# A quarter of one output projection moved behind the transposes, and the sample's projection parts joined in pairs

## The chip, the cores and the metric

The kernel runs on one core of one Trainium2 chip. The metric is the device time of one execution in microseconds (us); the median of three runs of the kernel before is 2836.79 us. Five engines work side by side, each in its own order: PE (matrix products, also transposes), DVE (vector), ACT (scalar), POOL (general), and SP, which here only issues the loads and stores (DMAs). They wait for each other by semaphores.

## The reference

One inference step of a one-layer decoder, all in fp32, for a prompt of 2048 tokens and a sample of 8 requests with 4 new tokens each (32 tokens). The width is 1024. Cut to what matters here:

```
y    = concatenate([o, s_out]) @ w_out          # o: gated linear attention, s_out: spatial gating
h    = x + y
q    = rmsnorm(h, g_x) @ wq_x                   # memory cross-attention, 4 heads, 256 memory tokens
h    = h + softmax(q @ mk.T / 16) @ mv @ wo_x   # mk, mv: from mem_prompt, or cache_mem_k/v for the sample
f    = (gelu(conv(rmsnorm(h, g_ffn) @ w_gate)) * (rmsnorm(h, g_ffn) @ w_up)) @ w_down     # d_ff 2816
h    = h + f
out  = rmsnorm(h, g_final)
```

`o` is normalized per head and multiplied by silu(r) before it enters `w_out`: rows 0 to 511 of `w_out` belong to `o`, rows 512 to 1023 to `s_out`.

## The kernel before

The 2048 prompt tokens are four sub-blocks of 512 (s = 0 to 3). The 32 sample tokens ride along with sub-block 1 through the mixer, so there T = 544, cut in two chunks of 272 columns. Activations lie transposed, 128 features by tokens; `B.h[0..7]` is the residual. Every fp32 product is three fp32r matmuls (`mm3`, L92 to L94): high times high, high times low, low times high. A weight unit is 512 KB, loaded raw by SP and split on chip by ACT (high part, L84) and DVE (low part, L85), unless it was prepared in DRAM before. Raw units share 5 buffers (`wraw`), split ones 5 each of high and low.

The work is a list of `Step`s, each with a function and the weight units that it reads. `weave` mixes main steps with side steps in proportion; `run` issues them in that order and asks for units 5 ahead (`AHEAD`). The Tile framework then schedules the instructions with a timeline of its own, so the final order on each engine can differ from the written one; the order of an engine's instructions is fixed when the program is built.

The change touches two places of sub-block 1.

*The output projection `wo`* (`out_proj_steps`). `half(m2, k0, last)` multiplies 4 of the 8 tiles of the reduction (from k0) for two of the 8 output tiles (m = 2·m2, 2·m2+1) and adds the result to `B.h[m]` (L1240). For sub-block 1 `first` is 4 and `second` is 0: the four halves with k0 = 4 read `s_out` and can run early; the four with k0 = 0 read `o`, and they finish a tile (`finish`: scaling wog L1250, the combinations t13, t24 and splits for the attention scores, the copy smpx for the sample L1260, squares on ACT L1262 and their sum on POOL L1267). The first list is woven with the tail of the linear attention (`gtail`, main steps 16 to 18: normalization of `o`, the gate L1181, `back`: transposes otp L1187 and, for the sample, otps L1192, each scaled and split into ch by ACT, L88, and cl by DVE, L89). The second list follows, then the statistics and the attention scores sc (matmuls into `sc10A..`, `sc10S..`, against splits of the finished pairs: w1, wth/wtl, wbh/wbl, wuh/wul with the number of the pair's odd tile, so `w1wo17` and `wthwo17` belong to tiles 6 and 7). Matmuls into `a_wo1<k0><m><chunk>` are these projections: `a_wo146x` and `a_wo147x` are the fourth half with k0 = 4, `a_wo100x` the first with k0 = 0.

*The sample's cross-attention* (`sample_steps`). Its steps run beside the feed-forward of sub-block 1 (main steps 1 to 37): project with `wq_x` ("sq"), then per request keys, scores, softmax, values, then project with `wo_x` ("so"). A projection is a sum over two halves j of the reduction for four column blocks m, in plain fp32 with 32x256 matmuls (L1406) into sqp or sop; each half reads one raw unit of 512 KB, `r_sq<m><j>` or `r_so<m><j>`. Raw units of the feed-forward, `r_wup1<j>S..`, share those buffers.

Of the kernel before, what the change touches and what calls it, by code (L numbers as in the profile page):

```python
# [37 lines left out]
def hymba_step_kernel(  # L38
# [22 lines left out]
    def U(name, dt=F32):  # L61
        return up.tile([128, TM], dt, tag="U", name=name)

    def T_(name, dt=F32):
        return tp_.tile([128, TM], dt, tag="T", name=name)
# [4 lines left out]
    def acc(name):  # L70
        return accp.tile([128, 512], F32, tag="acc", name=name)
# [7 lines left out]
    def const(shape, name, dt=F32):  # L79
        return cp.tile(shape, dt, tag=name, name=name)  # L80
# [10 lines left out]
    def mm3(ps, wh, wl, xh, xl, first, last):  # L91
        pe.matmul(ps, wh, xh, start=first, stop=False)  # L92
        pe.matmul(ps, wh, xl, start=False, stop=False)  # L93
        pe.matmul(ps, wl, xh, start=False, stop=last)  # L94
# [4 lines left out]
    def wload(w, k0, nk, m0, mw, name):  # L99
        raw = wraw(name)  # L100
        r3 = raw[:, :nk * mw].rearrange("p (k m) -> p k m", k=nk)
        nc.sync.dma_start(r3, w[k0 * 128:(k0 + nk) * 128, m0:m0 + mw].rearrange("(k p) m -> p k m", p=128))
        return r3
# [11 lines left out]
    def wraw_unit(*spec):  # L115
        return lambda: wload(*spec)
# [64 lines left out]
    def seven_tokens(a, b, H, name, apart=False):  # L181


        B11, B12, B21, B22 = a[:, :H], a[:, H:2 * H], b[:, :H], b[:, H:2 * H]
        t13, t24 = T_(f"t13{name}"), T_(f"t24{name}")
        lo_, hi_ = slice(0, H), slice(H, 2 * H)
        one = U(f"w1{name}", F32R)
        split(one[:, lo_], one[:, hi_], B11)
        out = {"A11": (one[:, lo_], one[:, hi_])}
        dve.tensor_tensor(t13[:, lo_], B12, B11, ALU.subtract)  # L190
        th, tl = U(f"wth{name}", F32R), U(f"wtl{name}", F32R)
        if apart:
            split(th[:, lo_], tl[:, lo_], t13[:, lo_])
        dve.tensor_tensor(t13[:, hi_], B22, B12, ALU.subtract)
        dve.tensor_tensor(t24[:, lo_], B22, t13[:, lo_], ALU.subtract)
        dve.tensor_tensor(t24[:, hi_], B21, t24[:, lo_], ALU.subtract)
        for nm, src, first, second in (("b", b, "A12", "S4"), ("u", t24, "S2", "A22"), ("t", t13, "S1", "S3")):
            if nm == "t":
                h, l, c = th, tl, slice(H if apart else 0, 2 * H)
            else:  # L200
                h, l, c = U(f"w{nm}h{name}", F32R), U(f"w{nm}l{name}", F32R), slice(0, 2 * H)
            split(h[:, c], l[:, c], src[:, c])
            out[first], out[second] = (h[:, lo_], l[:, lo_]), (h[:, hi_], l[:, hi_])
        return out
# [153 lines left out]
    for l in range(7):  # L358
        half = 1 << l
# [6 lines left out]
        m = const([128, 256], f"mask{l}", U8)  # L366
# [32 lines left out]
    def gcol(nm, k):  # L399
        return cols_of[nm][:, k:k + 1]  # L400
# [273 lines left out]
    def chunks_of(sample):  # L674
        return [(0, 272), (272, 272)] if sample else [(0, 512)]
# [535 lines left out]
    def out_proj_steps(B, unit, src, g, name, sample, first, finished, keep=None, seven=False,  # L1211
                       whole=False):

        s = B.s
        T = TM if finished else SB
        TH = SB if keep else T

        open_ = {}

        def half(m2, k0, last, begin=True, end=True):

            def fn(wu):
                wh, wl = wu
                x = src()
                if m2 == 0 and last:
                    B.hn, B.sq = [], None
                for mm in range(2):  # L1230
                    m = 2 * m2 + mm
                    ms = slice(mm * 128, (mm + 1) * 128)
                    for ci, (c0, cw) in enumerate(chunks_of(sample)):
                        cs = slice(c0, c0 + cw)
                        ps = acc(f"a_{name}{s}{k0}{m}{ci}") if begin else open_.pop(m)
                        for k in range(4):
                            mm3(ps[:, :cw], wh[:, k, ms], wl[:, k, ms], x[k0 + k][0][:, cs], x[k0 + k][1][:, cs],
                                begin and k == 0, end and k == 3)
                        if end:
                            dve.tensor_tensor(B.h[m][:, cs], ps[:, :cw], B.h[m][:, cs], ALU.add)  # L1240
                        else:
                            open_[m] = ps
                    if last:
                        finish(m)
            return Step(fn, [unit(k0, m2)])

        def finish(m):
            if seven:
                t = T_(f"{name}g{s}{m}")
                act.activation(t[:, :TH], B.h[m][:, :TH], AF.Copy, scale=gcol(g, m))  # L1250
                if m % 2:
                    B.hn.append(seven_tokens(B.even, t, TH // 2, f"{name}{s}{m}", name == "wo" and m == 7))
                else:
                    B.even = t
            else:
                hi, lo = U(f"{name}h{s}{m}", F32R), U(f"{name}l{s}{m}", F32R)
                split_scaled(hi[:, :TH], lo[:, :TH], B.h[m][:, :TH], gcol(g, m))
                B.hn.append((hi, lo))
            if keep:
                dve.tensor_scalar(keep()[:, m * NS:(m + 1) * NS], B.h[m][:, SB:TM], gcol(g, m), None, ALU.mult)  # L1260
            t = T_(f"{name}q{s}{m}")
            act.activation(t[:, :T], B.h[m][:, :T], AF.Square)  # L1262
            if m == 0:
                B.sq = U(f"{name}sq{s}")
                pool.tensor_copy(B.sq[:, :T], t[:, :T])
            else:
                pool.tensor_tensor(B.sq[:, :T], B.sq[:, :T], t[:, :T], ALU.add)  # L1267

        def stat():
            ps = mps(f"{name}ss{s}")  # L1270
            rs = narrow(f"{name}rs{s}")
            for c in range(5 if finished else 4):
                n = 128 if c < 4 else NS
                pe.matmul(ps[:n, c:c + 1], B.sq[:, c * 128:c * 128 + n], ones[:, 0:1], start=True, stop=True)
            rstd_of(rs[:, :4], ps[:, :4], 128, 4, 1.0 / D)
            if finished:
                rstd_of(rs[:NS, 4:5], ps[:NS, 4:5], NS, 1, 1.0 / D)
            B.rs = rs

        second = 4 - first  # L1280
        if whole:
            out = [half(m2, first, False, end=False) for m2 in (0, 1)]
            out += [half(m2, second, True, begin=False) for m2 in (0, 1)]
            for m2 in (2, 3):
                out += [half(m2, first, False, end=False), half(m2, second, True, begin=False)]
            return out[:2], out[2:], Step(stat)
        return ([half(m2, first, False) for m2 in range(4)], [half(m2, second, True) for m2 in range(4)], Step(stat))


    def attention_steps(B):  # L1290
# [93 lines left out]
    def sample_steps():  # L1384
# [12 lines left out]
        def project(w, of, got, name):  # L1397


            st = {}  # L1400

            def part(m, j, raw):
                if m % 2 == 0 and j == 0:
                    st["ps"] = mps(f"{name}p{m}")
                for k in range(4):
                    pe.matmul(st["ps"][hr[k], (m % 2) * 256:(m % 2 + 1) * 256], of(4 * j + k), raw[:, k],  # L1406
                              start=j == 0, stop=j == 1)
                if m % 2 and j:
                    t = T_(f"{name}t{m}")
                    dve.tensor_copy(t[:, :512], st["ps"])  # L1410
                    if m == 1:
                        st["f"] = mps(f"{name}f")
                    for i in range(4):
                        a = ((m // 2) * 4 + i) * NS
                        pe.matmul(st["f"][:, a:a + NS], t[:, i * 128:(i + 1) * 128], sum4, start=True, stop=True)
                    if m == 3:
                        got(st["f"])

            return [Step(lambda a, m=m, j=j: part(m, j, a), [wraw_unit(w, 4 * j, 4, m * 256, 256, f"{name}{m}{j}")])
                    for m in range(4) for j in range(2)]  # L1420

        def got_q(ps):
            smp.qs = U("sqs")
# [85 lines left out]
        out = []  # L1509
# [260 lines left out]
    for s, B in enumerate(blocks):  # L1770
# [6 lines left out]
        if B.mix_sample:  # L1777
            def keep():
                if not hasattr(smp, "x"):
                    smp.x = U("smpx")  # L1780
                return smp.x
        w1, w2, stat = out_proj_steps(B, lambda k0, m2, s=s: (w_out[0], k0, 4, m2 * 256, 256, f"wo{s}{k0}{m2}"),
                                      lambda B=B: B.cat, "gx", "wo", B.mix_sample, 4, B.mix_sample, keep, seven=True, whole=not B.mix_sample)
# [59 lines left out]
```

## Time and profile before

| | before |
|---|---|
| median of 3 runs (range) | 2836.79 us (2836.49 to 2840.41) |
| profiled execution | 2837.18 us |
| its span | 2835.5 us |
| PE busy | 2797.1 us (99%) |
| DVE, ACT, POOL busy | 1894.6 (67%), 1106.0 (39%), 569.5 us (20%) |
| mean granted PE clock | 0.995 |
| DMA | 638.21 MB, 225 GB/s in the mean |

Times in the profile count from the span's start. A timeline row gives start, duration, engine, line, operation, output <- inputs and, in brackets, the idle time before it with the instruction that ended it. A wait row reads "engine, output, line <- what ended the wait: total, times, longest". Matmuls overlap: a row's duration is longer than the distance to the next one, and the distance is what PE needs for it.

### The profile page before, as it was taken

How to read it: one execution, taken by the hardware profiler on the slowest of the kernel's cores; microseconds unless marked ns; L12 is line 12 of the kernel's file. 1: busy time of each engine (PE TensorE's matmuls, PEld its weight loads, DVE VectorE, ACT ScalarE, POOL GpSimd, SP SyncE). 2: the span in 40 equal slices, each digit the busy share in tenths (PEclk: the TensorE clock that was granted, in tenths of full speed). 3: DMA queues.
4: the chain of work that ended last, by engine and by line, in shares of the span. 5: the costliest groups of instructions: out<-in, count | busy, mean ns of one | idle time of the engine just before them, and what ended most of it. 6: DMA issues, size and time to landing. Idle time of an engine off the chain costs nothing.

```text
span 2835.5 us, 47052 instructions
## 1 busy us (share of the span) xinstructions
PE 2797.1 (99%) x17894; PEld 2477.9 (87%) x17894; DVE 1894.6 (67%) x3266; ACT 1106.0 (39%) x1950; POOL 569.5 (20%) x638
## 2 busy tenths in 40 slices
PE   8999999999999999999999999999999999999998
PEld 8888888888887898898888889899999888899997
DVE  6578778777657786655555778666666687665555
ACT  5645544333363354223124445422223544431222
POOL 2002213111111221322210121222221022132222
PEclk9999999999999999999999999999999999999999
DMA  9756589999932245888995216577776323677774
GB/s 297 250 182 219 180 267 341 336 343 329 337 112 68 85 154 195 314 288 291 331 324 190 82 60 208 194 252 258 258 269 207 112 69 128 206 260 273 272 281 177
DMA packets 369687, 638.21 MB, mean 225 GB/s; under 512 B 27370, under 2 KB 238412, under 8 KB 369462
## 3 DMA queue, kind: packets, MB, share of 16 engines
q1 hardware_dynamic: 369462, 635.20, 65.7%
q8 instruction: 142, 2.33, 0.3%
q14 instruction: 83, 0.68, 0.1%
HBM read 507.69 MB, written 127.41 MB: 224 GB/s over the span
## 4 chain that ended last, share of the span: by engine, by line
PE 63%; DVE 3%; ACT 1%; issue 0%; POOL 0%; DMA 0%; POOLq 0%; DVEq 0%; ACTq 0%
PE d L94 4%; PE d L92 4%; PE d L93 4%; PE a_wx L94 2%; PE a_wx L93 2%; PE a_wx L92 2%; PE a_wo L92 1%; PE s L1046 1%; PE a_wo L93 1%; PE a_wo L94 1%; PE a_wu L92 1%; PE a_wu L93 1%; PE t_wr L92 1%; PE t_wr L93 1%; PE a_wu L94 1%; PE t_wr L94 1%
## 5 line engine op out<-in xcount | busy, mean ns | idle before, releaser
L92 PE MATMUL d<-acth,whi_wd 128*128 128x272 f32 (+1 forms) x688 | 235.4, 342 | 0.0
L1692 DVE TENSOR_TENSOR h<-d,h 128x512 f32<-128x512 f32 (+1 forms) x232 | 133.7, 582 | 149.4 <-PE d L94 149.2
L94 PE MATMUL d<-acth,wlo_wd 128*128 128x272 f32 (+1 forms) x688 | 233.4, 340 | 0.0
L93 PE MATMUL d<-actl,whi_wd 128*128 128x272 f32 (+1 forms) x688 | 233.3, 339 | 0.0
L1589 POOL TENSOR_TENSOR c<-c,bc_f 128x512 f32<-128x512 f32 (+1 forms) x88 | 137.0, 1562 | 140.4 <-ACT c L1588 139.7
L1579 ACT ACTIVATE c<-g,colsb 128x512 f32<-128x512 f32 x88 | 71.7, 815 | 189.7 <-DVE g L1542 141.7
L94 PEld LDWEIGHTS d<-acth,wlo_wd 128*128 128x128 f32 x688 | 129.5, 188 | 15.5 <-issue 1.2
L93 PEld LDWEIGHTS d<-actl,whi_wd 128*128 128x128 f32 x688 | 129.5, 188 | 13.5 <-issue 0.4
L92 PEld LDWEIGHTS d<-acth,whi_wd 128*128 128x128 f32 x688 | 129.6, 188 | 13.1
L1611 POOL TENSOR_TENSOR c<-r_q_wup,c 128x512 f32<-128x512 f32 (+1 forms) x33 | 63.3, 1918 | 329.4 <-DVE r_q_wup L288 209.6
L92 PE MATMUL a_wo<-ch,h_wo 128*128 128x512 f32 (+1 forms) x320 | 114.3, 369 | 2.0 <-ACT r L876 1.3
L1576 POOL COPY carry<-g 128x2 f32<-128x2 f32 x88 | 29.5, 335 | 420.8 <-DVE g L1542 418.8
L93 PE MATMUL a_wo<-cl,h_wo 128*128 128x512 f32 (+1 forms) x320 | 113.8, 358 | 0.0
L94 PE MATMUL a_wo<-ch,l_wo 128*128 128x512 f32 (+1 forms) x320 | 112.9, 356 | 0.0
L1580 DVE SCALAR_TENSOR_TENSOR c<-g,colsb,c 128x512 f32<-128x512 f32 x88 | 84.9, 965 | 28.3 <-ACT c L1579 27.8
L94 PE MATMUL a_wx<-pTh,wlo_wx 128*128 128x512 f32 x256 | 101.3, 396 | 0.0
L93 PE MATMUL a_wx<-pTl,whi_wx 128*128 128x512 f32 x256 | 100.6, 393 | 0.0
L92 PE MATMUL a_wx<-pTh,whi_wx 128*128 128x512 f32 x256 | 100.2, 394 | 0.0
L84 ACT ACTIVATE acth<-c 128x512 fp32r<-128x512 f32 (+1 forms) x88 | 55.9, 637 | 109.6 <-DVE c L1611 78.0
L1588 ACT ACTIVATE c<-c 128x512 f32<-128x512 f32 (+1 forms) x88 | 56.1, 637 | 94.5 <-DVE c L1581 82.6
L1581 DVE SCALAR_TENSOR_TENSOR c<-g,colsb,c 128x512 f32<-128x512 f32 x88 | 90.6, 1029 | 1.1
L85 DVE TENSOR_TENSOR actl<-c,acth 128x512 fp32r<-128x512 f32 (+1 forms) x88 | 63.1, 720 | 26.6 <-ACT acth L84 25.6
(3753 smaller groups left out, 9741.8 us busy)
## 6 DMA issues: line engine op xcount, KB each, us to landing
whi_wd<-wd SPq DMA_DIRECT2D x66, 512.0 KB, 7.7
wlo_wd<-wd SPq DMA_DIRECT2D x66, 512.0 KB, 7.3
r_wo<-in_w_out_dram SPq DMA_DIRECT2D x32, 512.0 KB, 3.4
wlo_wx<-vod SPq DMA_DIRECT2D x32, 512.0 KB, 4.2
whi_wx<-vod SPq DMA_DIRECT2D x32, 512.0 KB, 5.0
r_wg<-in_w_gate_dram SPq DMA_DIRECT2D x22, 512.0 KB, 7.6
r_wup<-in_w_up_dram SPq DMA_DIRECT2D x22, 512.0 KB, 5.3
r_wd<-in_w_down_dram SPq DMA_DIRECT2D x22, 512.0 KB, 4.5
```

Of the source, the lines that this page charges most:

```text
L84: act.activation(hi, src, AF.Copy)
L85: (lo_eng or dve).tensor_tensor(lo, src, hi.bitcast(F32), ALU.subtract)
L92: pe.matmul(ps, wh, xh, start=first, stop=False)
L93: pe.matmul(ps, wh, xl, start=False, stop=False)
L94: pe.matmul(ps, wl, xh, start=False, stop=last)
L1579: act.activation(c[:, :SB], g[:, 2:SB + 2], AF.Identity, bias=cb, scale=w2)
L1580: dve.scalar_tensor_tensor(c[:, :SB], g[:, 1:SB + 1], w1, c[:, :SB], ALU.mult, ALU.add)
L1581: dve.scalar_tensor_tensor(c[:, :SB], g[:, 0:SB], w0, c[:, :SB], ALU.mult, ALU.add)
L1588: act.activation(c[:, :T], c[:, :T], AF.Gelu_apprx_tanh)
L1589: pool.tensor_tensor(c[:, :T], c[:, :T], B.fbc[:, :T], ALU.mult)
L1611: (dve, pool)[i].tensor_tensor(c[:, :T], q[i], c[:, :T], ALU.mult)
L1692: dve.tensor_tensor(B.h[m + mm][:, cs], ps[:, :cw], B.h[m + mm][:, cs], ALU.add)
```

## The change

In the first place the list of early halves loses its last entry (m2 = 3), which is put into the second list ahead of that list's last entry. In the second, the eight one-unit steps of each sample projection become four steps with two units each.

```diff
@@ out_proj_steps
-        return ([half(m2, first, False) for m2 in range(4)], [half(m2, second, True) for m2 in range(4)], Step(stat))
+        out = [half(m2, second, True) for m2 in range(4)]
+        out.insert(3, half(3, first, False))
+        return [half(m2, first, False) for m2 in range(3)], out, Step(stat)
@@ sample_steps, project
-            return [Step(lambda a, m=m, j=j: part(m, j, a), [wraw_unit(w, 4 * j, 4, m * 256, 256, f"{name}{m}{j}")])
-                    for m in range(4) for j in range(2)]
+            def parts(m, *raws):
+                for j, raw in enumerate(raws):
+                    part(m, j, raw)
+
+            return [Step(lambda *raws, m=m: parts(m, *raws),
+                         [wraw_unit(w, 4 * j, 4, m * 256, 256, f"{name}{m}{j}") for j in range(2)])
+                    for m in range(4)]
```

No arithmetic changes. The instructions of the three places that the prediction speaks of stand as follows; the last number in a name is only a counter.

PE at the transposes of the gated output in sub-block 1, before (the first rows of the fourth early half, `a_wo1460`, stand between the transposes of o12 and o13):

```order
L1157 MATMUL kvs11_9836<-v14_8942,km111_9607 64x128 x2
L1187 MATMUL otp10_10020<-ident_81,o12_9048 128x128
L92 MATMUL a_wo1460_10138<-ch14_9455,h_wo143_9653 128x272
L93 MATMUL a_wo1460_10138<-cl14_9456,h_wo143_9653 128x272
L94 MATMUL a_wo1460_10138<-ch14_9455,l_wo143_9654 128x272
L92 MATMUL a_wo1460_10138<-ch15_9549,h_wo143_9653 128x272
L93 MATMUL a_wo1460_10138<-cl15_9550,h_wo143_9653 128x272
L94 MATMUL a_wo1460_10138<-ch15_9549,l_wo143_9654 128x272
L92 MATMUL a_wo1460_10138<-ch16_9740,h_wo143_9653 128x272
L93 MATMUL a_wo1460_10138<-cl16_9741,h_wo143_9653 128x272
L94 MATMUL a_wo1460_10138<-ch16_9740,l_wo143_9654 128x272
L92 MATMUL a_wo1460_10138<-ch17_9755,h_wo143_9653 128x272
```

PE at the same place, after:

```order
L1157 MATMUL kvs11_9836<-v14_8942,km111_9607 64x128 x2
L1187 MATMUL otp10_10020<-ident_81,o12_9048 128x128
L1187 MATMUL otp10_10020<-ident_81,o13_9049 128x128
L92 MATMUL a_wo1000_10138<-ch10_10025,h_wo100_9653 128x272
L93 MATMUL a_wo1000_10138<-cl10_10026,h_wo100_9653 128x272
L94 MATMUL a_wo1000_10138<-ch10_10025,l_wo100_9654 128x272
L1192 MATMUL otps10_10029<-ident_81,o14_9050 128x32
L1187 MATMUL otp11_10033<-ident_81,o10_9046 128x128
L1187 MATMUL otp11_10033<-ident_81,o11_9047 128x128
L1187 MATMUL otp11_10033<-ident_81,o12_9048 128x128
L1187 MATMUL otp11_10033<-ident_81,o13_9049 128x128
L1192 MATMUL otps11_10042<-ident_81,o14_9050 128x32
```

The fourth early half is gone from here: the second transpose follows the first, and the first late half (`a_wo1000`) is the next product, reading ch10 and cl10, which come from these transposes. The `a_wo146x` and `a_wo147x` matmuls now stand between those of `a_wo1051` and `a_wo1060`.

DVE at the end of the projection, before (h1_6 and h1_7 are the last two tiles; the rows after the last addition prepare the last pair for the scores):

```order
L1240 TENSOR_TENSOR h1_6_7779<-a_wo1061_10499,h1_6_7779 128x272
L85 TENSOR_TENSOR wtlwo13_10366<-t13wo13_10359,wthwo13_10365 128x512
L85 TENSOR_TENSOR w1wo15_10456<-wog14_10418,w1wo15_10456 128x256
L196 TENSOR_TENSOR t24wo15_10455<-wog15_10452,t24wo15_10455 128x256
L1240 TENSOR_TENSOR h1_7_7780<-a_wo1070_10519,h1_7_7780 128x272
L1260 TENSOR_SCALAR smpx_10230<-h1_6_7779,colsb_658 128x32
L85 TENSOR_TENSOR wblwo15_10466<-wog15_10452,wbhwo15_10465 128x512
L1240 TENSOR_TENSOR h1_7_7780<-a_wo1071_10533,h1_7_7780 128x272
L1260 TENSOR_SCALAR smpx_10230<-h1_7_7780,colsb_658 128x32
L190 TENSOR_TENSOR t13wo17_10549<-wog16_10513 128x256
L85 TENSOR_TENSOR l_qk10S3_10482<-r_qk10S3_10479,h_qk10S3_10481 128x1024
L85 TENSOR_TENSOR wulwo15_10470<-t24wo15_10455,wuhwo15_10469 128x512
```

DVE at the same place, after:

```order
L1240 TENSOR_TENSOR h1_7_7780<-a_wo1470_10451,h1_7_7780 128x272
L1240 TENSOR_TENSOR h1_7_7780<-a_wo1471_10465,h1_7_7780 128x272
L85 TENSOR_TENSOR wulwo15_10408<-t24wo15_10393,wuhwo15_10407 128x512
L85 TENSOR_TENSOR l_qk10S2_10420<-r_qk10S2_10417,h_qk10S2_10419 128x1024
L1240 TENSOR_TENSOR h1_6_7779<-a_wo1060_10485,h1_6_7779 128x272
L85 TENSOR_TENSOR wtlwo15_10399<-t13wo15_10392,wthwo15_10398 128x512
L1240 TENSOR_TENSOR h1_6_7779<-a_wo1061_10499,h1_6_7779 128x272
L1260 TENSOR_SCALAR smpx_10168<-h1_6_7779,colsb_658 128x32
L1240 TENSOR_TENSOR h1_7_7780<-a_wo1070_10519,h1_7_7780 128x272
L85 TENSOR_TENSOR w1wo17_10551<-wog16_10513,w1wo17_10551 128x256
L1240 TENSOR_TENSOR h1_7_7780<-a_wo1071_10533,h1_7_7780 128x272
L1260 TENSOR_SCALAR smpx_10168<-h1_7_7780,colsb_658 128x32
```

The additions of the moved half (from `a_wo147x`) stand among those of the last late half, and splits of the earlier pair 15 (wulwo15, wtlwo15) and of w1wo17 stand ahead of the last addition now, where they followed it before.

SP near the end of the sample's output projection, before:

```order
L102 DMA r_so20_15109<-in_wo_x_dram 128x4x256
L148 DMA wg110S1_15119<-s7g10_213 128x1024
L148 DMA wg110S3_15121<-s7g10_213 128x1024
L102 DMA r_so21_15235<-in_wo_x_dram 128x4x256
L102 DMA r_so30_15248<-in_wo_x_dram 128x4x256
L148 DMA wg110S4_15125<-s7g10_213 128x1024
L148 DMA wg110A12_15123<-w7g10_212 128x1024
L148 DMA wg110A22_15233<-w7g10_212 128x1024
L148 DMA wup110A11_15255<-w7u10_214 128x1024
L210 DMA r_wup110S2_15257<-s7u10_215 128x1024
L210 DMA r_wup110S1_15263<-s7u10_215 128x1024
```

SP at the same place, after:

```order
L759 DMA x2_00_15579<-in_x_prompt_dram 128x512
L759 DMA x2_01_15582<-in_x_prompt_dram 128x512
L759 DMA x2_10_15585<-in_x_prompt_dram 128x512
L148 DMA wg110A22_15214<-w7g10_212 128x1024
L759 DMA x2_11_15588<-in_x_prompt_dram 128x512
L148 DMA wup110A11_15233<-w7u10_214 128x1024
L102 DMA r_so20_15229<-in_wo_x_dram 128x4x256
L102 DMA r_so21_15231<-in_wo_x_dram 128x4x256
L210 DMA r_wup110S2_15235<-s7u10_215 128x1024
L210 DMA r_wup110S1_15357<-s7u10_215 128x1024
L148 DMA wup110A22_15380<-w7u10_214 128x1024
```

The parts r_so20 and r_so21 are issued together just ahead of the two r_wup110S loads, and r_so10 and r_so11 (not shown) stand further back than before, nearer to them. The loads of the next sub-block's input x2 have moved behind them too. The query projection's loads change in the same way.

## The prediction

> **What bounds the kernel.** I read the page first.
>
> ```profile
> span 2835.5 us, 47052 instructions
> ...
> PE 2797.1 (99%) x17894; PEld 2477.9 (87%) x17894; DVE 1894.6 (67%) x3266; ACT 1106.0 (39%) x1950; POOL 569.5 (20%) x638
> ```
>
> PE is busy 2797.1 us of a span of 2835.5 us. The profiled execution took 2837.18 us, so 1.7 us lie around the span; it stands 0.39 us above the median of the three runs, 2836.79 us, to which I add the differences below. Only 38 us of the span are without PE work. A change that leaves PE's work as it is can win only from such gaps, or from stretches in which PE runs at a lower clock. So I read the busy time by stage around the change (columns: busy time of PE, weight loads, DVE, ACT, POOL; granted clock; DMA share; GB/s):
>
> ```profile
> ...
> 960.00:1030.00 70.00, 68.08 (x560) 61.95 (x552) 53.71 (x117) 29.96 (x49) 21.95 (x17) 1.00 0.36 114
> 1030.00:1075.00 45.00, 41.79 (x314) 40.36 (x315) 33.41 (x70) 21.05 (x40) 4.78 (x4) 0.92 0.59 203
> 1420.00:1500.00 80.00, 80.00 (x622) 69.75 (x621) 40.27 (x62) 20.72 (x41) 16.76 (x24) 1.00 0.94 343
> ```
>
> PE idles 1.92 us in the first stage (the last steps before attention), 3.2 us in the second (end of the projection and first scores), which also has a mean clock of 0.92, and not at all in the third, where the sample's output projection runs beside the feed-forward. The waits of the first two stages:
>
> ```profile
> ...
> PE sc10S L92 <- DVE h L1240: 1.7, 1, 1.7
> ...
> PE sc10A L92 <- ACT wbhwo L84: 0.8, 1, 0.8
> PE sc10S L92 <- ACT wthwo L84: 0.6, 1, 0.6
> PE sc10S L94 <- DVE wulwo L85: 0.4, 1, 0.4
> PE sc10A L92 <- DVE h L1240: 0.3, 1, 0.3
> ```
>
> These come at the first scores: 1.7 + 0.8 + 0.6 + 0.4 + 0.3 = 3.8 us. That is all the waiting there is behind the projection. The clock of that stage needs a closer look, so I cut stretches of 3.41 us around PE's gaps, the length in which the lower clock starts and ends in this trace:
>
> ```profile
> ...
> 252.40:255.82 3.42, 1.59 (x10) 1.26 (x10) 3.42 (x6) 0.20 (x1) 1.70 (x1) 1.00 0.21 74
> 286.54:289.95 3.41, 1.22 (x10) 0.74 (x9) 3.17 (x6) 1.41 (x2) 1.88 (x1) 1.00 0.94 284
> 289.95:296.78 6.83, 6.48 (x18) 4.71 (x18) 3.42 (x5) 2.42 (x4) 0.03 (x1) 0.50 0.66 243
> 1034.05:1037.46 3.41, 2.10 (x13) 1.48 (x11) 3.41 (x7) 2.80 (x7) 0.50 (x1) 1.00 0.09 23
> 1037.46:1044.29 6.83, 6.25 (x28) 5.96 (x28) 4.71 (x8) 2.90 (x5) 1.64 (x1) 0.50 0.20 68
> 1044.29:1051.12 6.83, 6.83 (x58) 6.65 (x57) 2.69 (x8) 1.64 (x2) 1.52 (x2) 1.00 0.57 200
> 1685.99:1689.40 3.41, 0.66 (x4) 0.42 (x4) 1.66 (x2) 0.43 (x1) 1.83 (x1) 1.00 0.40 112
> 1689.40:1692.82 3.42, 3.11 (x7) 2.48 (x8) 2.73 (x4) 1.99 (x4) 0.00 (x0) 0.50 0.10 42
> ```
>
> Three stretches with PE busy 1.22, 2.10 and 0.66 of 3.41 us are each followed at once by 6.83, 6.83 and 3.41 us at half clock; one with 1.59 us (252.40) is not. So a gap here costs its length, and often more: 6.83 us of busy PE at clock 0.50 is 3.4 us of work not done. The scores' gap is followed by such a stretch (1037.46), so its price is 3.8 + 3.4 = 7.2 us.
>
> **The change, part 1: the moved quarter.** It is 48 matmuls (4 of the reduction's tiles, 3 products, 2 column tiles, 2 chunks), 4 additions into h, one 512 KB load and one split. None is added or removed; they go from ahead of the transposes of the gated output to just ahead of the projection's last step.
>
> *Where it leaves.* These rows stand there:
>
> ```profile
> ...
> 994.45 1.06 ACT L84 ACTIVATE h_wo<-r_wo 128x1024 fp32r<-128x1024 f32 x1 [5.96 <-PE a_wo L93]
> ...
> 995.05 0.33 PE L1187 MATMUL otp<-ident,o 128*128 128x128 f32 x1
> ...
> 995.55 1.23 DVE L85 TENSOR_TENSOR l_wo<-r_wo,h_wo 128x1024 fp32r<-128x1024 f32 x1
> ...
> 996.69 0.67 DVE L1181 TENSOR_TENSOR o<-o,ors 32x512 f32<-32x512 f32 x1
> ...
> 997.03 0.69 ACT L88 ACTIVATE ch<-otp,colsb 128x512 fp32r<-128x512 f32 x1 [1.52 <-PE otp L1187]
> ...
> 997.75 0.75 DVE L89 SCALAR_TENSOR_TENSOR cl<-otp,colsb,ch 128x512 fp32r<-128x512 f32 x1
> ...
> 1001.44 0.24 PE L1192 MATMUL otps<-ident,o 32*128 32x32 f32 x1
> ```
>
> Two transposes stood 1.7 us apart with a third of the quarter between them, and the rest covered the chain otp, ch, cl until 1001.44. Now they run back to back at 995.1 and 995.2, and the next matmul reads ch. ACT is busy with h_wo until 994.45 + 1.06 = 995.51, then ch takes 0.69: 996.2. cl (0.75) follows the l_wo split, which ends at 995.55 + 1.23 = 996.8: 997.5. The sample's gate on o (0.67), which otps needs, comes behind cl on DVE now: 998.1. PE idles 0.85, 1.1 and 0.4 us between: 2.3 us. Below that it can't go under the 0.85 us, since ACT frees no earlier. From above I bound it by the same transposes in the next sub-block, which has no such cover:
>
> ```profile
> ...
> 1688.60 0.66 PE L1187 MATMUL otp<-ident,o 128*128 128x128 f32 x4 [2.86 <-DVE o L1181]
> ...
> 1689.71 1.22 PE L92 MATMUL a_wo<-ch,h_wo 128*128 128x512 f32 x2 [0.45 <-ACT ch L88]
> ```
>
> 2.86 + 0.45 = 3.3 us. I take 2.3, since its terms are rows of this place. The rest of the phase keeps its work: by the new order the transposes of the other heads and the second half's first matmuls are interleaved, as at 1001 to 1010 before, where PE did not wait. The split of the moved unit on DVE (1.23) and ACT (1.06) trades places with other units' splits, and its load goes three units later in SP's queue; no wait for a weight stands at either place, so I cost these at nothing.
>
> Does this gap bring the half clock? It would leave PE busy some 1.1 to 1.6 us of a stretch of 3.41, between the 1.22 that was followed by it and the 1.59 that was not, and it can also fall across two stretches. I count it as less likely than not.
>
> *Where it arrives.* The rows:
>
> ```profile
> ...
> 1011.00:1027.00 16.00, 16.00 (x130) 16.00 (x130) 15.96 (x32) 11.27 (x21) 7.52 (x5) 1.00 0.32 99
> 1009.58:1033.68 24.10, 22.12 (x173) 21.55 (x172) 24.06 (x47) 15.97 (x27) 10.18 (x7) 1.00 0.28 88
> ```
>
> ```profile
> ...
> L1240 DVE TENSOR_TENSOR h<-a_wo,h x16: 424/430/442, 1009.6 to 1033.3; 128x272 f32<-128x272 f32 x16
> ```
>
> ```profile
> ...
> L85 DVE TENSOR_TENSOR wtlwo<-t13wo,wthwo x5: 409/675/689, 1019.9 to 1040.6; 128x512 fp32r<-128x512 f32 x3, 128x256 fp32r<-128x256 f32 x2
> ...
> L194 DVE TENSOR_TENSOR t13wo<-wog,wog x4: 414/416/1564, 1013.3 to 1036.6; 128x256 f32<-128x256 f32 x4
> ```
>
> ```profile
> ...
> 1027.58 1.22 DVE L85 TENSOR_TENSOR l_qk10S<-r_qk10S,h_qk10S 128x1024 fp32r<-128x1024 f32 x1
> ...
> 1028.10 0.29 PE L94 MATMUL a_wo<-ch,l_wo 128*128 128x272 f32 x1
> ...
> 1031.60 0.72 ACT L1250 ACTIVATE wog<-h,colsb 128x512 f32<-128x512 f32 x1 [2.77 <-DVE wtlwo L85]
> ```
>
> PE makes 130 matmuls in 16.00 us, 0.123 each, so the quarter is 5.9 us. DVE has no gap (24.06 of 24.10 us) between the first addition of the finishing half (1009.58) and past the last (1033.25): DVE sets this stage, and the last addition starts 5.15 us after PE's last projection matmul at 1028.10. After the change the finishing half starts earlier: 1001.44 - 998.1 = 3.3 us, and 3 matmuls (0.4) of it are done ahead, so its first addition stands at 1005.9. DVE then has 23.7 us of the same rows, four more additions (4 x 0.43 = 1.7) and three splits of earlier pairs that now stand ahead of the last addition (0.69 + 0.69 + 0.41 = 1.8, by the row of wtlwo for 128x512 and 128x256), which brings that addition to 1033.1. PE ends the projection at 1028.1 + 2.3 = 1030.4. The lag falls from 5.15 to 2.7 us.
>
> Then PE has 38 matmuls of the scores that need only earlier pairs; at 6.83/58 = 0.118 us (the row of 1044.29) they last until 1034.9. The chain for the last pair is the addition 0.43, behind it the split l_qk10S 1.22 on DVE with the scaling wog 0.72 on ACT beside it, a combination of 0.42 on DVE (t13wo) and, estimated like it, 0.4 for the split on ACT and 0.65 for two small instructions between: 1033.1 + 3.1 = 1036.2. One wait of 1.3 us is left, against 3.8. It lies between 0 (DVE ahead by 1.3 us, no slow instance like the 1.56 us of t13wo before it) and 3.8 (DVE's lag unchanged). Gain 2.5 us. One wait of 1.3 us stands alone, where before three stood within 3 us behind another of 1.7; so I expect the half clock gone: 3.4 us more. PE keeps 2.1 us of such a stretch, though, and 2.10 brought it at 1034.05, so this is the weakest step.
>
> A page bears on this: the Trainium skill's "TensorE: Matmul & The Clock Gate", in "What's actually happening", says that the clock falls to half after an idle window of about 3.4 us and comes back after a busy one. The trace agrees on the length and on the two levels, but not on the idle window: at 1034.05 PE was busy 2.10 of 3.41 us and the half clock came. By the page's wording no gap of 2.3 us could lower the clock, so by it the sum below stays at its likeliest case, 2833.7 us, and the rival with a half clock falls away.
>
> **Part 2: sample parts in pairs.** The 128 fp32 matmuls and 16 loads of 512 KB are the same; the sample's 66 steps in the feed-forward become 58, spread over the same main steps, and each pair's loads are issued together. In FFN PE never waits before, so nothing is to be won. What can be lost is a late feed-forward weight, since SP issues in order:
>
> ```profile
> ...
> 1462.21 2.48 SPq L210 DMA_DIRECT2D r_wup110S<-s7u  x2
> ```
>
> ```profile
> ...
> SPq L102 <- PE sop L1406: 5.5, 1, 5.5
> ```
>
> ```profile
> ...
> L92 PE MATMUL a_wup110S<-wthwx,h_wup110S x8: 274/282/286, 1479.4 to 1482.6; 128*128 128x256 f32 x8
> ...
> L84 ACT ACTIVATE h_wup110S<-r_wup110S x2: 1059/1060/1062, 1470.6 to 1471.9; 128x1024 fp32r<-128x1024 f32 x2
> ```
>
> ```profile
> ...
> r_wup<-in_w_up_dram SPq DMA_DIRECT2D x22, 512.0 KB, 5.3
> ```
>
> Before, the two r_wup110S loads were issued at 1462.21 and about 1464.4, and SP stood 5.5 us behind them for a buffer that sop frees. Now the second of them stands behind such a wait, for a later part of sop: up to 1464.4 + 5.5 plus the second part of the pair, some 1470.5. It is first needed at about 1477.6 (1479.4 before, less what the pairing moves behind it). With the page's median of 5.3 us and the split 1.06 it is there at 1476.9; with the 7.5 us of before (1464.4 to 1471.9) at 1479.1, 1.5 us late, and its low half, split on DVE, can be as late again. So 0 to 3 us; the queue has drained behind the wait, so I take 0.5 for this and the like place at the query projection together.
>
> **Sum:** +2.3 - 2.5 - 3.4 + 0.5 = -3.1 us: 2836.8 - 3.1 = 2833.7 us. About 0.2% (5.7 us) is what a measurement of this kernel can tell from no change.
>
> **Rivals.**
> - *A half clock comes after all*, behind the front gap or still at the scores: +3.4, so 2837.1 us. For it: the stretches at 286.54 and 1034.05. Against: 252.40.
> - *The last stage stays bound by DVE* (the other side: slower). The 3.8 us of waits and their half clock stay, while the front gap is paid: +2.3 + 0.5 = 2839.6, and with the half clock in front too 2843.0. It decides if the last addition still starts 5 us after PE's last projection matmul. For it: DVE has 24.06 of 24.10 us. Against: the additions of 5.9 us of PE work are only 1.7 us.
> - *The end is freed wholly and the front costs only 0.85*: -3.8 - 3.4 + 0.85 = -6.3, 2830.5 us.
> - *The late weight*: 3 us instead of 0.5, 2836.2.
>
> **Chances.** Likeliest case 0.42; one half clock 0.26; DVE-bound end 0.14, half of it with the front's half clock; wholly freed 0.11; late weight 0.07. Faster by over 0.2% is the wholly freed case alone, 0.11; slower by over 0.2% the worse half of the DVE-bound case, with a little for sums of misses, 0.08; within it 0.81. Leaving those two out, the range goes from 2831 (front at 1.2, end freed) to 2841 (DVE-bound end with the front at its 3.3 us): some 8 in 10.
>
> **What would show it.** Right: about 998 us a wait `otp` or `otps<-DVE` and `a_wo<-ACT ch`, 2.3 us in all; the first scores' waits under 1.5 us; no half clock between 1030 and 1050; no PE wait from 1075 to 1500. Wrong: a stretch at clock 0.50 after 998; the `sc10` waits still near 3.8; a wait on h_wup110S or h_wup11S.

## The result, and the profile after

The change made the kernel a little slower: 2840.08 us against 2835.96 us (medians of 14 runs each), ratio 1.0016 with a 95% interval of 1.0008 to 1.0023, so +4.5 us (2.3 to 6.5). The ratio leaves out one slow run on each side (7065.73 us before, 3034.89 us after), which the medians hold. Forecast were 2833.7 us, a range of 2831 to 2841, and a gain of 3.1 us. The time is inside the range, the sign is wrong. The first lines of the page after:

```profile
span 2838.0 us, 47054 instructions
...
PE 2793.9 (98%) x17894; PEld 2476.2 (87%) x17894; DVE 1894.3 (67%) x3266; ACT 1106.2 (39%) x1950; POOL 572.8 (20%) x638
```

The span is 2.5 us longer and PE's busy time 3.2 us shorter, so PE idles 5.7 us more: the loss is waiting, not work. PE's waits (total, times, longest) from the last steps of the projection to the scores:

```profile
...
PE a_wo L93 <- DVE cl L89: 0.8, 1, 0.8
PE a_wo L92 <- ACT ch L88: 0.8, 1, 0.8
PE sc10A L94 <- DVE w1wo L85: 0.7, 1, 0.7
PE sc10S L94 <- DVE wtlwo L85: 0.5, 1, 0.5
PE a_wo L92 <- DVE h L1240: 0.4, 1, 0.4
```

Where the front waits stand (start, duration, ..., idle before and its end):

```profile
...
996.38 0.39 PE L92 MATMUL a_wo<-ch,h_wo 128*128 128x272 f32 x1 [0.78 <-ACT ch L88]
997.59 0.39 PE L93 MATMUL a_wo<-cl,h_wo 128*128 128x272 f32 x1 [0.82 <-DVE cl L89]
```

The two front waits on ch and cl are there (0.8 + 0.8, and 0.4 at the additions), and the scores wait 0.7 + 0.5 = 1.2 us where they waited 3.8. PE's waits in the feed-forward of the sub-block, where there was none before:

```profile
...
PE a_wg19A L92 <- DMA wg19A<-w7g: 2.7, 1, 2.7
PE a_wup110S L92 <- ACT h_wup110S L84: 1.9, 1, 1.9
PE sof L1417 <- DVE sot L1412: 0.5, 1, 0.5
PE a_wup11A L92 <- DMA wup11A<-w7u: 0.4, 1, 0.4
```

2.7 + 1.9 + 0.5 + 0.4 = 5.5 us, 5.1 of them between 1420 and 1500. The stretches (busy PE, weight loads, DVE, ACT, POOL; granted clock; DMA share; GB/s):

```profile
...
1030.00:1075.00 45.00, 43.76 (x365) 43.17 (x364) 34.83 (x74) 22.49 (x46) 4.37 (x4) 1.00 0.68 233
1420.00:1500.00 80.00, 74.77 (x592) 66.83 (x591) 40.55 (x59) 20.31 (x39) 17.51 (x25) 0.96 0.94 336
1471.19:1474.60 3.41, 1.03 (x8) 0.62 (x6) 2.53 (x4) 3.10 (x4) 2.06 (x4) 1.00 0.21 74
1474.60:1481.43 6.83, 6.83 (x41) 5.50 (x41) 5.10 (x5) 1.95 (x4) 2.48 (x2) 0.50 0.96 325
```

The clock of the score stage is 1.00 (it was 0.92), and a half clock of 6.83 us has turned up in the feed-forward instead, at 1474.6, behind a stretch with PE busy 1.03 of 3.41 us. To keep the stages apart I take three marks in sub-block 1 from each trace: PE's first projection matmul (a_wo), its first transpose of the attention weights (pT), and the first spatial-gating product of the next sub-block (zp). "First and last start" are the columns behind the durations. Before:

```profile
...
L92 PE MATMUL a_wo<-ch,h_wo x128: 283/288/396, 961.8 to 1027.8; 128*128 128x272 f32 x128
```

```profile
...
L1374 PE MATMUL pT<-ident,p x16: 271/273/273, 1064.0 to 1068.5; 128*128 128x128 f32 x16
```

```profile
...
L916 PE MATMUL zp<-wsT,sv x32: 273/275/276, 1637.7 to 1668.3; 128*128 128x128 f32 x32
```

After:

```profile
...
L92 PE MATMUL a_wo<-ch,h_wo x128: 282/288/394, 962.0 to 1031.1; 128*128 128x272 f32 x128
```

```profile
...
L1376 PE MATMUL pT<-ident,p x16: 270/272/273, 1060.6 to 1065.1; 128*128 128x128 f32 x16
```

```profile
...
L916 PE MATMUL zp<-wsT,sv x32: 270/275/275, 1640.5 to 1671.1; 128*128 128x128 f32 x32
```

From a_wo to pT it is 102.2 us before and 98.6 after: 3.6 us won. From pT to zp it is 573.7 before and 579.9 after: 6.3 us lost (in unrounded starts). In the two profiled executions the rest differs by 0.1 us ahead of a_wo and 0.3 us behind zp.

### The profile page after: what moved, and what is told of

It is laid out like the page before. It is cut to its first block, busy times and chain, and to the rows that moved or that the text cites. A ratio compares the mean times of both kernels' runs of the same rounds, so it can differ in the third digit from the quotient of the medians.

```text
span 2838.0 us, 47054 instructions
## 1 busy us (share of the span) xinstructions
PE 2793.9 (98%) x17894; PEld 2476.2 (87%) x17894; DVE 1894.3 (67%) x3266; ACT 1106.2 (39%) x1950; POOL 572.8 (20%) x638
## 4 chain that ended last, share of the span: by engine, by line
PE 61%; DVE 4%; DMA 1%; ACT 1%; issue 1%; POOL 0%; SPq 0%; POOLq 0%; ACTq 0%; DVEq 0%
PE d L94 4%; PE d L92 4%; PE d L93 4%; PE a_wx L93 2%; PE a_wx L94 2%; PE a_wx L92 2%; PE s L1046 1%; PE a_wo L92 1%; PE a_wu L92 1%; PE a_wu L93 1%; PE t_wr L92 1%; PE a_wu L94 1%; PE t_wr L93 1%; PE t_wr L94 1%; PE a_wo L93 1%
## 5 line engine op out<-in xcount | busy, mean ns | idle before, releaser
L93 PE MATMUL a_wx<-pTl,whi_wx 128*128 128x512 f32 x256 | 100.5, 392 | 0.0
L92 PE MATMUL a_wx<-pTh,whi_wx 128*128 128x512 f32 x256 | 100.1, 393 | 0.0
```

## The experiments

My theory after the result, T1: the two parts act apart; the moved quarter wins in front of the scores, and the loss comes from the paired output projection of the sample, whose loads crowd the feed-forward's weights. Rivals: R1, the feed-forward merely starts at another time against its loads; R2, the half clock comes back elsewhere. The ratios below are to the kernel before, timed alongside, with 95% intervals.

**The moved quarter alone.**

```diff
 # out_proj_steps as in the change, sample_steps as before
```

> The first part of the change alone: the quarter is moved, the sample's projections stay as before. Theory T1 (the two parts act apart, the loss is that of the paired output projection): the front waits of 0.8 + 0.8 + 0.4 = 2.0 us come, the scores' waits fall from 3.8 to about 1.2 us and the half clock of 6.83 us at 1037 goes (3.4 us), no wait of PE from 1075 to 1500: 4.0 us faster than before, about 0.14%. Rival R1 (the feed-forward's weights are late because the feed-forward starts at another time against its loads): a wait of 2 to 3 us on wg19A here too, and no gain, 0 to 4 us slower. Rival R2 (the half clock comes back elsewhere, since it follows any gap in some share of executions): the waits as T1 has them, but only 0.6 us faster.

Measured: ratio 1.0002 (0.9994 to 1.0011), median 2836.78 us against 2835.38. No wait of PE between 1075 and 1500, front and score waits as in the change. So R1 falls; but the 4.0 us that T1 expected aren't there in the median either, though this profiled execution was 3.4 us shorter than the one of before. The interval (1.7 us faster to 3.1 us slower) leaves T1's gain out and has room for R2's 0.6 us. Its stretches:

```profile
...
994.49:997.90 3.41, 1.73 (x10) 1.03 (x9) 2.95 (x5) 1.25 (x3) 0.00 (x0) 1.00 0.71 175
997.90:1001.31 3.41, 3.41 (x16) 2.70 (x14) 1.82 (x4) 1.72 (x5) 0.00 (x0) 0.50 0.91 284
1030.00:1075.00 45.00, 43.79 (x365) 43.20 (x364) 34.90 (x74) 22.16 (x46) 4.36 (x4) 1.00 0.68 225
```

Here the front gap (PE busy 1.73 of 3.41 us) brought a half clock of 3.41 us, which in the change's own profile the same gap did not.

**The output projection alone in pairs.**

```diff
-            return [Step(lambda a, m=m, j=j: part(m, j, a), ...)]
+            # "so": one step with two units per m, as in the change; "sq": as before
```

> Only the sample's output projection (wo_x) in pairs; the quarter and the query projection stay as before. T1: the waits wg19A (2.7), h_wup110S (1.9) and sof (0.5) come between 1420 and 1500, and a half clock of 6.83 us behind them (3.4): 5 to 8.5 us slower, 0.2 to 0.3%. R1: no such waits, within 1 us of before.

Measured: 1.0022 (1.0013 to 1.0031), 6.2 us slower, median 2841.99 against 2835.38.

```profile
...
PE a_wup110S L92 <- ACT h_wup110S L84: 1.9, 1, 1.9
PE a_wg19A L92 <- DMA wg19A<-w7g: 1.1, 1, 1.1
PE sof L1415 <- DVE sot L1410: 0.5, 1, 0.5
```

The same three waits, 3.5 us, and a half clock of 6.83 us behind them. So the loss comes from this part. Its median stands further above the kernel before than that of the whole change, but the intervals overlap.

**The query projection alone in pairs.**

```diff
+            # "sq": one step with two units per m, as in the change; "so": as before
```

> Only the sample's query projection (wq_x) in pairs. T1: one wait of about 0.4 us near 1170 and nothing else, within 1 us of before. Rival R3 (any pairing delays the K and V loads and with them the feed-forward's weights): waits of 2 us or more between 1120 and 1500, 2 to 5 us slower.

Measured: 1.0006 (0.9997 to 1.0015): no difference that can be told. One wait came, on a key load (R3 asks for waits of 2 us or more, at weights too):

```profile
...
PE kTp L1460 <- DMA kc<-in_cache_mem_k_dram: 1.3, 1, 1.3
```

**One tile of the quarter instead of two.**

```diff
-        return ([half(m2, first, False) for m2 in range(4)], [half(m2, second, True) for m2 in range(4)], Step(stat))
+        out = [half(m2, second, True) for m2 in range(4)]
+        out.insert(3, one(7, first))                        # one(m, k0): half() for one tile, a unit of 256 KB
+        return [half(m2, first, False) for m2 in range(3)] + [one(6, first)], out, Step(stat)
```

> The sample's projections as before; of the moved quarter only one of its two output tiles (24 matmuls, 2.9 us) goes to the end, the other stays ahead of the transposes, each with a load of 256 KB of its own. T1 with the reading that about 2.9 us of work is enough to cover the chain otp, ch, cl: no front wait over 0.5 us, the scores' waits between 1.2 and 2.5 us, no half clock at 1037: 4.5 to 6 us faster than before, 0.5 to 2 us faster than the first part alone. Rival R4 (the scores' half clock goes only when the whole quarter is at the end): 1 to 2 us faster than before.

Measured: 0.9997 (0.9988 to 1.0005).

```profile
...
PE sc10A L92 <- ACT wuhwo L84: 0.8, 1, 0.8
PE sc10S L92 <- DVE h L1240: 0.4, 1, 0.4
PE sc10A L94 <- DVE w1wo L85: 0.3, 1, 0.3
```

The front wait is gone wholly, 1.5 us are left at the scores, and neither place has a half clock: the stage from a_wo to pT takes 97.4 us, 4.8 us less than in the profile of before. The gain in the medians, 0.9 us (3.4 faster to 1.4 slower), is less than T1 forecast, and no change lies inside its interval. By the time, R4 (1 to 2 us faster) is not ruled out; what R4 rests on, a half clock that stays at the scores, is not in this profile.

**The pairs with their old spacing.**

```diff
-            return [Step(lambda *raws, m=m: parts(m, *raws), [... two units ...]) for m in range(4)]
+            return [s2 for m in range(4) for s2 in (Step(lambda *raws, m=m: parts(m, *raws), [... two units ...]),
+                                                     Step(lambda: None))]
```

> Only the sample's output projection in pairs, but an empty step behind each pair, so that the sample has its 66 steps again and the K and V loads keep their places beside the feed-forward. Theory Ts (the loss is the spacing: 58 steps on the same main steps put the V loads and all of the output projection's loads later, into the stretch where the loads are already dense): no wait over 0.5 us between 1420 and 1500, within 1 us of before. Rival Tp (the loss is the pair itself: two units at once out of five raw buffers and five units of lead): the waits on wg19A or h_wup110S of 1 to 3 us stay, 4 to 7 us slower than before.

Measured: 0.9999 (0.9991 to 1.0008), against 1.0022 without the empty steps. The only wait of PE in the feed-forward:

```profile
...
PE xt L778 <- ACT sdo L1437: 0.3, 1, 0.3
```

The time agrees with Ts and not with Tp: two units in one step cost nothing that can be told when an empty step follows; fewer steps do. Ts is right about the spacing, but what it says of the loads needs a closer look. The weave spreads 58 steps in the change (62 with this pair alone) over the main steps that 66 shared, so the eight loads of wo_x are used in the last 4 of 58 instead of the last 8 of 66. The issues of these loads, and PE's products that read them, in the profile before, in the change and here (behind the colon the durations, then first and last start):

```profile
...
L1406 PE MATMUL sop<-r_so,sos x64: 378/380/404, 1438.2 to 1479.9; 128*32 128x256 f32 x64
L102 SPq DMA_DIRECT2D r_so<-in_wo_x_dram x8: 383/384/1207, 1397.2 to 1470.2; - x8
```

```profile
...
L1408 PE MATMUL sop<-r_so,sos x64: 379/379/636, 1459.9 to 1489.5; 128*32 128x256 f32 x64
L102 SPq DMA_DIRECT2D r_so<-in_wo_x_dram x8: 378/384/538, 1427.1 to 1476.1; - x8
```

```profile
...
L1406 PE MATMUL sop<-r_so,sos x64: 379/379/403, 1436.3 to 1468.1; 128*32 128x256 f32 x64
L102 SPq DMA_DIRECT2D r_so<-in_wo_x_dram x8: 383/470/946, 1396.1 to 1453.5; - x8
```

Eight loads of 512 KB went out over 73 us before, over 49 us in the change, and over 57 us here, but from 1396 on, as before. Here the last one goes out 17 us earlier than before, so the empty steps do not bring back the old places wholly. In the change the first load goes out 30 us later, the last 6 us, and the first product comes 22 us later. Does that crowd the feed-forward's loads? The stretches before and after:

```profile
...
1420.00:1430.00 10.00, 10.00 (x74) 7.74 (x72) 2.34 (x4) 0.38 (x1) 0.00 (x0) 1.00 0.73 240
1430.00:1440.00 10.00, 10.00 (x90) 8.79 (x87) 3.59 (x7) 0.00 (x0) 0.88 (x1) 1.00 1.02 349
```

```profile
...
1420.00:1430.00 10.00, 9.91 (x82) 8.48 (x81) 2.06 (x4) 0.39 (x1) 0.00 (x0) 1.00 0.93 312
1430.00:1440.00 10.00, 8.96 (x76) 8.75 (x74) 7.19 (x10) 3.54 (x5) 1.81 (x1) 1.00 1.05 384
```

The DMA share of 1420 to 1430 rises from 0.73 to 0.93, but where PE starts to wait (busy 8.96 of 10) it is 1.05 against 1.02 before, and there PE did not wait. So the share does not explain the wait; the times do. Counted from pT, the wg19A load that PE waits for landed at 380.9 us in the change and at 380.7 before (by its semaphore in the trace): it was not late. PE came to it early, at 378.4 instead of 381.2 us. In the eleven traces of this document the load landed between 380.0 and 381.8 us; the three runs that wait for it (the change, the pairs alone, and the run with an earlier end below) are the three in which no product with wo_x has run by then, and PE is there at 378.4 to 379.2 us. In the eight others 14 or 16 of the 64 have run, PE is there at 381.2 to 382.6 us, and none waits. Before the change the load had landed only 0.5 us ahead of PE.

The wait on h_wup110S has another cause again. ACT, which splits that weight, before and in the change:

```profile
...
1470.59 1.06 ACT L84 ACTIVATE h_wup110S<-r_wup110S 128x1024 fp32r<-128x1024 f32 x1 [2.74 <-DMA r_wup110S<-s7u]
```

```profile
...
1471.50 0.81 ACT L1586 ACTIVATE c<-g,colsb 128x512 f32<-128x512 f32 x1 [4.66 <-DVE g L1549]
1472.22 1.99 ACT L84 ACTIVATE h_wup110S<-r_wup110S 128x1024 fp32r<-128x1024 f32 x2
```

Before, ACT waited for the load and split it. In the change the loads had landed at 1469.3 and 1471.0, but an instruction of the feed-forward's convolution (c<-g) now stands ahead of the split, and it waited for DVE until 1471.5. PE, ready at 1471.4, had to wait until 1473.3. With the pairs alone the order is the same, and the first load landed so late (1473.0) that a part of the wait, some 0.6 us, would have come without it. With the empty steps the split stands ahead of c<-g as before. Why the framework orders ACT in this way isn't known.

**The pairs, ending two main steps earlier.**

```diff
-            sides.append((sample_steps(), 1, len(fmain) - 5))
+            sides.append((sample_steps(), 1, len(fmain) - 7))    # only "so" in pairs, 62 steps
```

> The output projection in pairs and 62 steps, ending two main steps of the feed-forward earlier (at the 35th instead of the 37th). Ts: the loads are back about where they were, no wait over 0.5 us at the weights, within 1.5 us of before. Tp: waits of 1 to 3 us at feed-forward weights, one or two units earlier than in the change, 4 to 7 us slower.

Measured: 1.0005 (0.9996 to 1.0013).

```profile
...
PE a_wup19S L92 <- ACT h_wup19S L84: 1.4, 1, 1.4
PE a_wg19A L92 <- DMA wg19A<-w7g: 0.9, 1, 0.9
PE a_wup19S L94 <- DVE l_wup19S L85: 0.3, 1, 0.3
```

The time can't be told from that of before, but the interval (1.1 us faster to 3.7 slower) has room for the waits, and they stay: 2.6 us at weights one unit earlier, without a half clock behind them. So the waits are of the kind that Tp expects, and the time is the one of Ts. The loads go out from 1394.1 to 1453.3, as with the empty steps, and PE waits for wg19A all the same, from 1441.3 to 1442.2, since its products with wo_x start behind it:

```profile
...
L1406 PE MATMUL sop<-r_so,sos x64: 379/379/404, 1443.7 to 1465.0; 128*32 128x256 f32 x64
```

So late loads are not needed for that wait. The r_wup19S loads were late: SP stood 5.8 us at a load of wo_x for a buffer that sop frees, and issued them at 1444.9 and 1446.1 (1438.1 and 1438.8 with the empty steps). Here the pairs held up the queue.

**The front gap filled.**

```diff
+            if sample and h == 0:                       # in back(), behind the transposes of the first head
+                fl = mps("fill")
+                for i in range(16):
+                    pe.transpose(fl[:, :128], B.o[3][:, 384:512], ident)
```

> The first part alone (moved quarter), with 16 transposes of 128x128 more on PE, whose result nothing reads, between the second transpose and the first product that waits for ch: they fill 1.7 of the 2.0 us that PE waits there. Theory Th (a gap of PE brings the half clock in some of the executions, by where it falls in the 3.41 us stretches): the front waits fall under 0.9 us, never a half clock between 990 and 1005, and the median is 0.5 to 1.5 us under that of the first part alone, 2834.5 to 2836 at a median of before of 2835.4. Rival: the extra transposes add their 1.7 us to the time, 2838.

Measured: 0.9997 (0.9988 to 1.0006), median 2833.29 us against 2834.72; the first part alone had 1.0002. The scores' waits are those of the first part alone (0.7 and 0.6 us). At the front are left:

```profile
...
PE a_wo L92 <- DVE h L1244: 0.4, 1, 0.4
PE otps L1196 <- DVE o L1181: 0.2, 1, 0.2
```

16 transposes more cost nothing that can be told, and the front waits fall to 0.6 us without a half clock in this profile. That agrees with Th; that the median is lower by the half clock alone isn't settled, since the intervals overlap.

**The whole change with its spacing kept.**

```diff
 # the change, with Step(lambda: None) behind each of the eight pairs
```

> The whole change, with an empty step behind each of the eight pairs, so that the sample has its 66 steps again. Ts: no wait over 0.5 us between 1075 and 1500; front and score waits as in the first part alone; the time is that of the first part alone or a little less, 2833 to 2837, 3 to 6 us under the change as it was. Rival Ti (the moved quarter and the pairs disturb each other, since the feed-forward starts 3.4 us earlier against its loads): a wait on wg19A of 1 to 3 us stays, 2838 or more.

Measured: 0.9999 (0.9990 to 1.0008), median 2835.52 us; the change had 1.0016.

```profile
...
994.00:997.41 3.41, 1.74 (x12) 0.87 (x8) 3.19 (x6) 1.37 (x2) 0.00 (x0) 1.00 0.62 158
997.41:1000.82 3.41, 3.41 (x15) 2.82 (x14) 1.40 (x4) 1.84 (x4) 0.00 (x0) 0.50 0.96 295
1420.00:1500.00 80.00, 79.77 (x637) 71.04 (x636) 42.70 (x72) 24.14 (x47) 19.48 (x25) 1.00 0.97 347
```

PE is busy 79.77 of 80 us from 1420 to 1500, against 74.77 in the change, and that at a DMA share of 0.97, against 0.94. Ti falls: with their spacing kept, the parts don't disturb each other. The front gap brought its half clock here as well.

**One tile moved, and pairs with their spacing.**

```diff
 # out_proj_steps as in the run with one tile; "so" in pairs with Step(lambda: None) behind each, "sq" as before
```

> One output tile of the moved quarter at the end instead of two, as in the run with the eighth, and the sample's output projection in pairs with an empty step behind each. From both alone (ratios 0.9997 and 0.9999): no front wait, score waits of about 1.5 us, no half clock at either place, no wait in the feed-forward: 1 to 4 us faster than before, 2831 to 2834. Rival: the gains are the noise of the half clock elsewhere, within 0.5 us of before.

Measured: 0.9989 (0.9980 to 0.9998), median 2832.09 against 2835.84 us: about 3 us under the kernel before (0.6 to 5.7). The scores' waits are the three of the run with one tile. The margin is thin, since one tile alone and the spaced pairs alone had 0.9997 and 0.9999, and the kernel with the change was not timed alongside.

**All traces side by side.** The half clock at the two places depends on the execution, so I compare the stages of all eleven profiles (us from mark to mark; the half clock at the front or the scores in this stage, and the one in the feed-forward):

| kernels | a_wo to pT | half clock in it | pT to zp | half clock in it |
|---|---|---|---|---|
| before | 102.2 | 6.83 at the scores | 573.7 | none |
| o pairs; q pairs; o spaced; o early | 100.1; 102.2; 100.5; 100.4 | none; 6.83; 3.41; 3.41 at the scores | 579.3; 573.9; 572.0; 573.6 | 6.83; none; none; none |
| change | 98.6 | none | 579.9 | 6.83 |
| quarter alone; change spaced | 100.0; 100.1 | 3.41; 3.41 at the front | 574.2; 572.9 | none |
| quarter, gap filled | 98.7 | none | 575.3 | none |
| one tile; one tile with spaced pairs | 97.4; 97.3 | none | 574.6; 573.9 | none |

With the projection as before the first stage has a mean of 101.1 us over five profiles; with the quarter moved 99.6 over three. In these profiles the moved quarter is worth about 1.5 us, and one tile of it about 3.7. The pairs in their late place cost about 6: 579.3 and 579.9 against 572.0 to 575.3 in the nine others. -1.5 + 6 agrees with the +4.5 that was measured. The 6 is borne out by the time of the pairs alone (6.2 us); the 1.5 is not, since the quarter alone took 1.0002 of the time of before, with 1.7 us faster and 3.1 us slower both inside the interval.

## Why the prediction was wrong

- **What bounds the kernel**: right. PE's work was unchanged, and all that moved the time was waits and half clocks.
- **Front gap, +2.3**: right. Its two main waits came to 1.6 us of 1.95 forecast. The third, 0.4 us at otps, did not come; that one of 0.4 came at the additions instead, which makes 2.0 in all, is luck; the chain otp, ch, cl ran as written (PE resumed at 996.4 and 997.6; forecast 996.2 and 997.5).
- **Score waits, -2.5**: right, 3.8 to 1.2 us. The working on DVE's lag was less good: the last addition starts 3.7 us after PE's last projection matmul (1031.4), not 2.7. The additions of h after:

```profile
...
L1240 DVE TENSOR_TENSOR h<-a_wo,h x20: 425/429/442, 1005.9 to 1035.1; 128x272 f32<-128x272 f32 x20
L1260 DVE TENSOR_SCALAR smpx<-h,colsb x8: 229/238/1341, 1007.3 to 1035.5; 128x32 f32<-128x32 f32 x8
```

```profile
...
1033.72 1.45 DVE L85 TENSOR_TENSOR w1wo<-wog,w1wo 128x256 fp32r<-128x256 f32 x1 [1.36 <-ACT w1wo L84]
```

  The first addition came at 1005.9 as forecast, the last at 1035.1 instead of 1033.1: w1wo took 1.45 us and one smpx 1.34, the slow instances that the bounds had allowed for. PE had other score matmuls for most of that time, and waited 0.7 us for this w1wo.
- **Half clock at the scores, -3.4**: mis-sized, and I had called it the weakest step. The half clock came in four of the five profiles with the old tail, for 6.83, 6.83, 3.41 and 3.41 us; at half speed that is 10.2 us in five, 2.0 us on average. The profile of before showed one of the longer ones, and I priced the change by it. The same gamble returned in front: two of three profiles with the moved quarter have 3.41 us of it at the front gap, 1.1 us on average. So by these profiles the two half clocks together were worth about 0.9 us, not 3.4.
- **Part 2, +0.5**: the step that failed and turned the sign; the term was about 6 us. I asked only whether a load comes later, for the second r_wup110S load, and took a value near the lower end of 0 to 3, because the queue would have drained behind its wait. Counted from pT, that load was issued 5.9 us later than before, as forecast (6.1), and PE did not wait for it. What I had wrong is the time at which PE needs the weights. I had counted "the 66 steps become 58, spread over the same main steps" as harmless, but it moved the sample's products with wo_x 22 us back, so that fewer of the sample's products run ahead of these weights. PE reached wg19A 2.8 us sooner, where 0.5 us was to spare: 2.7 us of waiting at a place I had not looked at. The 1.9 us at h_wup110S came at the first of the two loads, needed at 1477.0 before (the row that I read, 1479.4, is the second's), and from ACT's new order rather than from the load. The gap at 1471 then brought 6.83 us of half clock, for which the term had nothing. The DMA share of 0.94 in the row 1420 to 1500 would not have told: with the spacing kept it is 0.97, and PE does not wait.
- **The rivals**: the late weight was named, but priced at 3 us without a half clock. None of them put both on the feed-forward, and none had PE come early. That the time lies inside the range is luck: the end at 2841 was built from a DVE-bound end of the projection, which did not come.

## What to carry to other kernels

A step that merges others also changes how side work is spread: before joining steps, see which loads it delays, and which weights lose the side work that ran ahead of them and gave their loads time to land; here an empty step behind each pair kept the time. Cover moved from one gap opens another: here half of the moved work closed the far gap nearly as well (waits of 1.5 us against 1.2) and left the near one covered. A gap of PE is priced by an average over executions of the half clock that may follow it, not by the one execution in the profile.

## What the hardware showed

The half clock follows stretches of 3.41 us with little work of PE, and they need not be idle: in the eleven profiles every such stretch with a PE busy share up to 0.41 was followed by it, none above 0.61, and between them some were and some weren't (0.51 at 994 brought it twice, 0.53 at 1027 not). The Trainium skill's "TensorE: Matmul & The Clock Gate" ("What's actually happening") speaks of an idle stretch; the measurement goes further. The stretches lie on a grid that starts elsewhere in each execution, so the same gap of 2 us falls into one stretch or is shared by two; one or two stretches at half clock follow. The part ahead of a_wo, which no edit touches, took 959.8 us in the profile that has no half clock there behind its first 20 us (one tile), and 964.3 in the one that has 10.24 us of it (q pairs); the 33 runs of the kernel before that go with the first four experiments spread from 2831.29 to 2839.42 us; how much of that spread the half clock makes isn't shown.
